# One-stream SwiGLUs with a normalized operand of 256 columns from the tenth pair, two passes in the last, and operands at multiples of 256 bytes

## The chip, the cores and the metric

One NeuronCore of one Trainium2 chip runs the whole program in a single launch. The metric is device microseconds of one execution.

## The reference, cut to what matters

A stream x of 256 tokens by 1,024 channels and a context of 256 tokens go through two layers. Layer 0: a half-step SwiGLU on both streams, a mixer (windowed attention and a gated linear attention), a half-step SwiGLU on x alone. Layer 1: SwiGLU, pooling mixer, SwiGLU, all on x alone. So there are four SwiGLUs, the first with two streams, the second, third and fourth with one:

```
modulate(z, g, shift, scale) = rmsnorm(z, g) * (1 + scale) + shift
a, u   = split(modulate(x, ...) @ wi)      # wi: 1024 x 5632
x      = x + 0.5 * gate * ((silu(a) * u) @ wo)   # wo: 2816 x 1024
```

Shift, scale and gate are rows of `silu(c) @ w_mod + b_mod`, nine per layer. Everything is float32.

## The kernel before, in words

Channels lie on the partitions, tokens along the free dimension. A float32 product is made of float32r ones: each operand is split into a rounded part (hi, or X0) and the rest (lo, or X1), and hi·X0 + hi·X1 + lo·X0 is summed in PSUM. `weight` (line 138) loads a block of weights into `t_raw` on SP's queue, casts it to `t_hi` on ScalarE (144) and subtracts to get `t_lo` on VectorE (145); there are four buffers of each.

The first product of a SwiGLU runs in 22 *pairs*: pair p has two weight blocks of 128 x 1,024, one for a and one for u, and each goes through eight k-blocks of 128 channels. Three functions issue these matmuls:

- `product` (323): three matmuls of 258 columns per k-block. The operand `t_xA` holds x·(1 + scale)·g, not yet divided by its rms, in rows of 260 columns (NS); columns 256 and 257 hold the shift. After the pair `scaled` (375) multiplies both PSUM results by `t_rstd`, and `swiglu` (366, 367) adds the shift's products.
- `wide` (343 to 345): three matmuls of 512 columns, for two streams side by side.
- `merged` (337, 338): two passes. One matmul of 512 columns, hi·[X0 | X1], and one of 256, lo·X0, added onto the second half; `residual` adds the halves up. The second product of the one-stream SwiGLUs and the mixer's output use it.

`parts` (370, 371) splits the result into `t_g`, the operand of the second product: eight output blocks n, each over 22 k-blocks.

The first SwiGLU does the pairs in halves. In its second half it uses a *normalized* operand: `normalize` (298 to 304) multiplies two channel blocks by rstd on VectorE, scales and shifts on ScalarE, casts and subtracts into a `paired_tile`, whose k-blocks are 520 columns apart. `wide` then needs no `scaled`.

Beside this, `mod_dot` (174) computes the modulation rows with one VectorE dot per 128 rows of `w_mod`. How many dots a pair or an output block takes is set by the tables RATES0 to RATES3 through `step_mod` (187), which also issues their loads. The order of each engine's instructions is that of a scheduler in the tile framework, which places them by priority and dependence; each engine then runs its list in order.

Of the kernel before, what the change touches and what calls it, by code (L numbers as in the profile page):

```python
# [106 lines left out]
class Body:  # L107
# [270 lines left out]
    def ffn(self, l, wi, wo, Xs, rstds, gate, streams, nxt, rates, first=None):  # L378
# [7 lines left out]
        if first is None:
            cmg, gp = self.open(f"g{self.uid}", "right")
            self.modpool = gp
        for h in range(nh):
            G = None if first is not None and h == 0 else self.t(gp, [128, pph, 2, W], F32R, "g")  # L390
            split = first is not None and h == 0
            if split:
                cme, ep = self.open("early", "right")
                early = [self.t(ep, [128, 2, T], F32) for _ in range(pph)]
                begin, weights, pair, during, second, norm = first
                nf = begin(early)
                self.step_mod(rates[0][0])
                w = weights(nf)
                for p in range(nf, pph):
                    ps = [self.bank(), self.bank()]  # L400
                    pair(p, w, ps)
                    if p + 1 < pph:
                        w = weights(p + 1)
                    for q in (0, 1):
                        nc.scalar.copy(early[p][:, q, :], ps[q][:, :T])
                    during(p)
                    self.step_mod(rates[0][0])
                rstds = second()
                cmg, gp = self.open(f"g{self.uid}")
                self.modpool = gp  # L410
                G = self.t(gp, [128, pph, 2, W], F32R, "g")
            for j in range(pph):
                p = h * pph + j
                w = [self.weight(wi[p, i], 1024) for i in (0, 1)]
                if first is not None and not split:
# [11 lines left out]
                for i in range(ns):  # L427
                    self.step_mod(rates[h][1] / ns if 0 < j < pph - 1 else 0)
                    if i == 0 and split:
                        continue  # L430
                    c = slice(i * T, (i + 1) * T)
                    ps = [self.bank(), self.bank()]
                    for q in (0, 1):
                        self.product(ps[q], w[q], Xs[i])
                    if callable(rstds):
                        rstds = rstds()
                    za = self.scaled(gp, ps[0], rstds[i], T + 1, "za")
                    zu = self.scaled(gp, ps[1], rstds[i], T + 1, "zu")
                    if split:
                        e = early[p]  # L440
                        be = self.t(gp, [128, 2], F32, "be", 2)
                        for q in (0, 1):
                            nc.scalar.copy(be[:, q:q + 1], ps[q][:, T + 1:T + 2])
# [816 lines left out]
```

## Time and profile before

| | |
|---|---|
| median of 3 runs | 1169.08 us (1167.88 to 1169.91) |
| profiled execution, its own time | 1165.99 us |
| its span, first to last instruction | 1163.8 us |
| mean granted TensorE clock | 0.998 |
| busy share: PE, PEld, VectorE, ScalarE | 98%, 89%, 81%, 49% |

PE is TensorE's matmuls, PEld its weight loads, DVE is VectorE, ACT ScalarE, SP the engine whose queue issues the DMAs. Matmuls are pipelined, so that their durations overlap; L328 is line 328 of the kernel before.

### The profile page before, as it was taken

How to read it: one execution, taken by the hardware profiler on the slowest of the kernel's cores; microseconds unless marked ns; L12 is line 12 of the kernel's file. 1: busy time of each engine (PE TensorE's matmuls, PEld its weight loads, DVE VectorE, ACT ScalarE, POOL GpSimd, SP SyncE). 2: the span in 40 equal slices, each digit the busy share in tenths (PEclk: the TensorE clock that was granted, in tenths of full speed). 3: DMA queues.
4: the chain of work that ended last, by engine and by line, in shares of the span. 5: the costliest groups of instructions: out<-in, count | busy, mean ns of one | idle time of the engine just before them, and what ended most of it. 6: DMA issues, size and time to landing. Idle time of an engine off the chain costs nothing.

```text
span 1163.8 us, 19972 instructions
## 1 busy us (share of the span) xinstructions
PE 1142.5 (98%) x7658; PEld 1039.4 (89%) x7658; DVE 946.0 (81%) x1690; ACT 574.1 (49%) x937; POOL 10.0 (1%) x32
## 2 busy tenths in 40 slices
PE   7999999999999999999999999999999999999997
PEld 5999988888888899787999998899999889999986
DVE  6899799788758889776998878989887989966564
ACT  4647544232234464565555544545554455555543
POOL 0000000000000200000000000000000000000000
PEclk9999999999999999999999999999999999999999
DMA  8866557667755435311678767978776876655562
GB/s 341 296 249 226 160 186 232 201 200 264 249 162 194 167 108 176 118 66 60 236 265 266 253 205 249 321 268 303 255 256 193 301 251 230 219 182 177 150 185 87
DMA packets 74546, 247.45 MB, mean 213 GB/s; under 512 B 8273, under 2 KB 8913, under 8 KB 74194
## 3 DMA queue, kind: packets, MB, share of 16 engines
...
q14 instruction: 36, 0.29, 0.1%
...
## 4 chain that ended last, share of the span: by engine, by line
PE 92%; DVE 5%; DMA 1%; ACT 1%; issue 1%; SPq 0%; DVEq 0%; ACTq 0%
PE t_mm L330 15%; PE t_mm L329 15%; PE t_mm L328 15%; PE t_mm L337 11%; PE t_mm L343 7%; PE t_mm L345 7%; PE t_mm L344 7%; PE t_mm L338 6%; PE t_mm L582 3%; PE t_mm L903 1%; PE t_mm L876 1%; DVE t_lo L145 1%; PE t_mm L893 1%; DMA t_raw<-wi0k 1%; PE t_mm L626 1%
## 5 line engine op out<-in xcount | busy, mean ns | idle before, releaser
L144 ACT CAST t_hi<-t_raw 128x1024 fp32r<-128x1024 f32 (+1 forms) x344 | 326.6, 951 | 416.7 <-PE t_mm L329 175.1
L328 PE MATMUL t_mm<-t_xA,t_hi 128*128 128x258 f32 (+1 forms) x1536 | 437.4, 285 | 3.3 <-DVE t_x L929 2.1
L330 PE MATMUL t_mm<-t_xA,t_lo 128*128 128x258 f32 (+1 forms) x1536 | 437.6, 285 | 1.6 <-DVE t_lo L145 1.6
L329 PE MATMUL t_mm<-t_xA,t_hi 128*128 128x258 f32 (+1 forms) x1536 | 434.8, 283 | 0.1
L145 DVE TENSOR_TENSOR t_lo<-t_raw,t_hi 128x1024 fp32r<-128x1024 f32 (+1 forms) x344 | 376.6, 1097 | 70.9 <-ACT t_hi L144 70.0
L328 PEld LDWEIGHTS t_mm<-t_xA,t_hi 128*128 128x128 f32 x1536 | 292.3, 191 | 6.5 <-DVE t_x L929 2.4
L329 PEld LDWEIGHTS t_mm<-t_xA,t_hi 128*128 128x128 f32 x1536 | 291.3, 190 | 2.3 <-issue 1.4
L330 PEld LDWEIGHTS t_mm<-t_xA,t_lo 128*128 128x128 f32 x1536 | 290.9, 189 | 2.0 <-DVE t_lo L145 2.0
L174 DVE CUSTOM_DVE_ANT_0 t_junk<-t_rawm,t_x 128x1024 bf16<-128x1024 f32 x142 | 181.7, 1279 | 16.4 <-DMA t_rawm<-wmod 15.6
L337 PE MATMUL t_mm<-t_g,t_hi 128*128 128x512 f32 x528 | 185.8, 394 | 0.0
L338 PE MATMUL t_mm<-t_g,t_lo 128*128 128x256 f32 x528 | 147.5, 279 | 0.0
L337 PEld LDWEIGHTS t_mm<-t_g,t_hi 128*128 128x128 f32 x528 | 99.0, 187 | 23.4
L338 PEld LDWEIGHTS t_mm<-t_g,t_lo 128*128 128x128 f32 x528 | 99.1, 188 | 0.0
L343 PE MATMUL t_mm<-t_xA,t_hi 128*128 128x512 f32 x176 | 69.7, 396 | 0.0
L345 PE MATMUL t_mm<-t_xA,t_lo 128*128 128x512 f32 x176 | 69.6, 396 | 0.0
L344 PE MATMUL t_mm<-t_xA,t_hi 128*128 128x512 f32 x176 | 69.2, 393 | 0.0
L343 PE MATMUL t_mm<-t_g,t_hi 128*128 128x512 f32 x176 | 68.6, 390 | 0.0
L344 PE MATMUL t_mm<-t_g,t_hi 128*128 128x512 f32 x176 | 68.5, 389 | 0.0
L345 PE MATMUL t_mm<-t_g,t_lo 128*128 128x512 f32 x176 | 68.5, 389 | 0.0
L375 DVE TENSOR_TENSOR t_zu<-t_mm,t_rstd 128x257 f32<-128x257 f32 x66 | 27.9, 425 | 28.8 <-PE t_mm L330 28.6
L366 ACT ACTIVATE t_za<-t_za 128x256 f32<-128x256 f32 x77 | 38.6, 508 | 14.5 <-DVE t_za L375 14.4
L174 DVE CUSTOM_DVE_ANT_0 t_junk<-t_w,t_x 128x1024 bf16<-128x1024 f32 x32 | 41.0, 1281 | 4.6 <-DMA t_w<-wmod 2.9
...
## 6 DMA issues: line engine op xcount, KB each, us to landing
...
```

Source lines behind the costliest of these rows:

```text
L144: nc.scalar.copy(hi[:, :n], raw[:, :n])
L145: self.mark = nc.vector.tensor_tensor(lo[:, :n], raw[:, :n], hi.bitcast(F32)[:, :n], op=ALU.subtract)
L174: self.nc.vector.tensor_tensor_reduce(out=junk, in0=w, in1=self.srow[s], scale=0.5 if half else 1.0, scalar=b, op0=ALU.mult, op1=ALU.add, ...
L328: nc.tensor.matmul(ps[:, :n], hi[:, c], X[:, 0, k, :n], start=(k == 0), stop=False)
L329: nc.tensor.matmul(ps[:, :n], hi[:, c], X[:, 1, k, :n], start=False, stop=False)
L330: nc.tensor.matmul(ps[:, :n], lo[:, c], X[:, 0, k, :n], start=False, stop=(k == KB - 1))
L337: nc.tensor.matmul(ps, hi, X.rearrange("p x t -> p (x t)"), start=first, stop=False)
L338: nc.tensor.matmul(ps[:, T:], lo, X[:, 0], start=False, stop=last)
L343: nc.tensor.matmul(ps, hi, X0, start=first, stop=False)
L344: nc.tensor.matmul(ps, hi, X1, start=False, stop=False)
L345: nc.tensor.matmul(ps, lo, X0, start=False, stop=last)
L366: self.silu = self.nc.scalar.activation(za, za, AF.Silu, bias=ba)
```

## The change

`ffn` is split into `ffn_two` (the first SwiGLU, its work as before) and `ffn_one` (the others). In `ffn_one` pairs 0 to 8 use `product` as before. During pairs 0 to 3 the operand is also normalized, two k-blocks a pair, into a `paired_tile`. From pair 9 (OLD) on the normalized operand is used: in the second and third SwiGLU with `wide` on 256 columns, in the fourth (fold) with `merged`, whose halves are then added by a ScalarE copy and a VectorE add. Silu and the product follow without rstd or shift. Modulation dots start at pair 5 at 1.35 a pair (0.9 in the fourth), and 1.4 go to an output block. The `paired_tile` is packed: its k-blocks lie 512 columns (2,048 bytes) apart instead of 520. A pad of 24 columns in the pool of `t_g` moves that tile: in the built program of before it starts 96 bytes past a multiple of 256, now at a multiple of 256. In the first SwiGLU `t_g` starts at a multiple of 256 in both.

```diff
-RATES1 = ((0, 0.85, 1.8),)
-RATES2 = ((0, 0.85, 1.8),)
-RATES3 = ((0, 0.9, 0),)
+RATES = ((1.35, 1.4), (1.35, 1.4), (0.9, 0))
+OLD = 9
+GPAD = 24
...
     def paired_tile(self):
         f = self.t(self.xp, [128, 2 * KB * NS], F32R, "xA", 2)
-        return f.rearrange("p (k n) -> p k n", k=KB)[:, :, :2 * T].rearrange("p k (x t) -> p k x t", t=T)
+        return f[:, :2 * KB * T].rearrange("p (k x t) -> p k x t", k=KB, t=T)
...
+    def ffn_one(self, l, wi, wo, cur, gate, nxt, rates, fold):
+        nc = self.nc
+        cmg, gp = self.open(f"g{self.uid}", "right")
+        self.modpool = gp
+        G = self.t(gp, [128, NP, 2, T], F32R, "g")
+        self.t(gp, [128, GPAD], F32, "pad")
+        for p in range(NP):
+            w = [self.weight(wi[p, i], 1024) for i in (0, 1)]
+            self.step_mod(rates[0] if OLD - 4 <= p < NP - 1 else 0)
+            ps = [self.bank(), self.bank()]
+            if p < OLD:
+                for q in (0, 1):
+                    self.product(ps[q], w[q], cur.X[0])
+                if p == 0:
+                    r = cur.stats()[0]
+                    XN = self.paired_tile()
+                za = self.scaled(gp, ps[0], r, T + 1, "za")
+                zu = self.scaled(gp, ps[1], r, T + 1, "zu")
+                self.swiglu(za[:, :T], za[:, :T], zu[:, :T], za[:, T:T + 1], zu[:, T:T + 1])
+                self.parts(G, p, slice(0, T), za[:, :T])
+                if p < KB // 2:
+                    self.normalize([XN[:, 2 * p:2 * p + 2, i] for i in (0, 1)], gp, 0, 2 * p, r, cur.A[0], cur.B[0])
+                continue
+            za = self.t(gp, [128, T + 1], F32, "za", 2)[:, :T]
+            if fold:
+                zu = self.t(gp, [128, T + 1], F32, "zu", 2)[:, :T]
+            for q in (0, 1):
+                for k in range(KB):
+                    c = slice(k * 128, (k + 1) * 128)
+                    hi, lo = w[q][0][:, c], w[q][1][:, c]
+                    if fold:
+                        self.merged(ps[q], hi, lo, XN[:, k], k == 0, k == KB - 1)
+                    else:
+                        self.wide(ps[q][:, :T], hi, lo, XN[:, k, 0], XN[:, k, 1], k == 0, k == KB - 1)
+                if fold:
+                    z = (za, zu)[q]
+                    nc.scalar.copy(z, ps[q][:, :T])
+                    nc.vector.tensor_tensor(z, z, ps[q][:, T:], op=ALU.add)
+            self.silu = nc.scalar.activation(za, za if fold else ps[0][:, :T], AF.Silu)
+            nc.vector.tensor_tensor(za, za, zu if fold else ps[1][:, :T], op=ALU.mult)
+            self.parts(G, p, slice(0, T), za)
+        nxt.begin()
...
-        self.ffn(0, a["wi1"], a["wo1"], cur.X, cur.stats, 8, (0,), nxt, RATES1)
+        self.ffn_one(0, a["wi1"], a["wo1"], cur, 8, nxt, RATES[0], False)
...
-        self.ffn(1, a["wi2"], a["wo2"], cur.X, cur.stats, 2, (0,), nxt, RATES2)
+        self.ffn_one(1, a["wi2"], a["wo2"], cur, 2, nxt, RATES[1], False)
...
-        self.ffn(1, a["wi3"], a["wo3"], nxt.X, nxt.stats, 8, (0,), fin, RATES3)
+        self.ffn_one(1, a["wi3"], a["wo3"], nxt, 8, fin, RATES[2], True)
```

Where instructions move. VectorE's list in the second SwiGLU, before, from the conversion of pair 4's first weight (`t1121_lo`) to that of its second (`t1124_lo`); `t1083_za` and `t1084_zu` are pair 0's, `t1093_za` and `t1094_zu` pair 1's:

```order
L145 TENSOR_TENSOR t1121_lo_5948<-t1119_raw_5946,t1120_hi_5947 128x1024
L214 SCALAR_TENSOR_TENSOR t1082_rstd_t_5708<-t1082_rstd_t_5708,t1080_rv_5705 128x256
L201 SCALAR_TENSOR_TENSOR t1332_x_7269<-t816_x_4396,t4_x_78 128x1
L215 SCALAR_TENSOR_TENSOR t1081_rstd_5707<-t1082_rstd_t_5708,t1081_rstd_5707 128x256
L375 TENSOR_TENSOR t1083_za_5720<-t1077_mm_5653,t1081_rstd_5707 128x257
L375 TENSOR_TENSOR t1084_zu_5722<-t1078_mm_5654,t1081_rstd_5707 128x257
L375 TENSOR_TENSOR t1093_za_5790<-t1091_mm_5740,t1081_rstd_5707 128x257
L375 TENSOR_TENSOR t1094_zu_5792<-t1092_mm_5741,t1081_rstd_5707 128x257
L145 TENSOR_TENSOR t1124_lo_5954<-t1122_raw_5952,t1123_hi_5953 128x1024
```

The same list of the changed kernel, up to the conversion of pair 4's second weight, now `t1126_lo` (its first, `t1123_lo`, stands 11 rows ahead of the first row here). `t1107_za` is pair 2's, `t1118_za` and `t1119_zu` are pair 3's, L297 and L303 are the multiply and the subtraction of `normalize`:

```order
L370 TENSOR_TENSOR t1068_g_5636<-t1096_za_5798,t1068_g_5636 128x256
L297 TENSOR_TENSOR t1109_xt_5882<-t5_x_80,t1082_rstd_5708 128x512
L303 TENSOR_TENSOR t1084_xA_5721<-t1098_xt_5806,t1084_xA_5721 128x2x256
L366 SCALAR_TENSOR_TENSOR t1107_za_5874<-t1108_zu_5876,t1107_za_5874 128x256
L374 TENSOR_TENSOR t1118_za_5950<-t1116_mm_5900,t1082_rstd_5708 128x257
L374 TENSOR_TENSOR t1119_zu_5952<-t1117_mm_5901,t1082_rstd_5708 128x257
L370 TENSOR_TENSOR t1068_g_5636<-t1107_za_5874,t1068_g_5636 128x256
L297 TENSOR_TENSOR t1120_xt_5958<-t5_x_80,t1082_rstd_5708 128x512
L366 SCALAR_TENSOR_TENSOR t1118_za_5950<-t1119_zu_5952,t1118_za_5950 128x256
L303 TENSOR_TENSOR t1084_xA_5721<-t1109_xt_5882,t1084_xA_5721 128x2x256
L145 TENSOR_TENSOR t1126_lo_5972<-t1124_raw_5970,t1125_hi_5971 128x1024
```

The conversion has moved behind pair 3's `t_zu` and behind the normalizing of pairs 0 to 2.

PE's list in the fourth SwiGLU at the step from pair 8 to pair 9, before:

```order
L328 MATMUL t2009_mm_10997<-t1877_xA_10256,t2005_hi_10989 128x258
L329 MATMUL t2009_mm_10997<-t1877_xA_10256,t2005_hi_10989 128x258
L330 MATMUL t2009_mm_10997<-t1877_xA_10256,t2006_lo_10990 128x258
L328 MATMUL t2019_mm_11068<-t1877_xA_10256,t2013_hi_11055 128x258
L329 MATMUL t2019_mm_11068<-t1877_xA_10256,t2013_hi_11055 128x258
L330 MATMUL t2019_mm_11068<-t1877_xA_10256,t2014_lo_11056 128x258
```

And of the changed kernel:

```order
L327 MATMUL t2012_mm_11069<-t1869_xA_10242,t2008_hi_11061 128x258
L328 MATMUL t2012_mm_11069<-t1869_xA_10242,t2008_hi_11061 128x258
L329 MATMUL t2012_mm_11069<-t1869_xA_10242,t2009_lo_11062 128x258
L336 MATMUL t2021_mm_11138<-t1922_xA_10521,t2016_hi_11127 128x512
L337 MATMUL t2021_mm_11138<-t1922_xA_10521,t2017_lo_11128 128x256
```

From pair 9 on, a k-block takes two matmuls and two weight loads instead of three, on another `t_xA` tile.

## Rows read from the trace of the kernel before

**Rows 1.** The page, busy time: us, share of the span, number of instructions.

```profile
PE 1142.5 (98%) x7658; PEld 1039.4 (89%) x7658; DVE 946.0 (81%) x1690; ACT 574.1 (49%) x937; POOL 10.0 (1%) x32
```

**Rows 2.** The page, the chain that ended last, shares of the span by engine and by line.

```profile
PE 92%; DVE 5%; DMA 1%; ACT 1%; issue 1%; SPq 0%; DVEq 0%; ACTq 0%
PE t_mm L330 15%; PE t_mm L329 15%; PE t_mm L328 15%; PE t_mm L337 11%; PE t_mm L343 7%; PE t_mm L345 7%; PE t_mm L344 7%; PE t_mm L338 6%; PE t_mm L582 3%; PE t_mm L903 1%; PE t_mm L876 1%; DVE t_lo L145 1%; PE t_mm L893 1%; DMA t_raw<-wi0k 1%; PE t_mm L626 1%
```

**Rows 3.** The waits of PE from 556 to 1160 us: us in total, times, the longest.

```profile
PE t_mm L260 <- DVE t_ss L276: 1.4, 1, 1.4
PE t_mm L1162 <- ACT t_sq L1147: 1.3, 1, 1.3
PE t_mm L328 <- ACT t_xA L319: 1.2, 3, 0.5
PE t_mm L330 <- DVE t_lo L145: 0.4, 1, 0.4
```

**Rows 4.** Line 343 on PE in the first SwiGLU (the first matmul of three in `wide`), from 150 to 260 us and from 200 to 340 us: count, duration in ns (least, median, most), first and last start in us. `t_g` in the second product's first half, `t_xA` in the first product's second half.

```profile
L343 PE MATMUL t_mm<-t_g,t_hi x88: 388/389/398, 150.6 to 209.8; 128*128 128x512 f32 x88
...
L343 PE MATMUL t_mm<-t_xA,t_hi x176: 387/396/400, 210.5 to 332.5; 128*128 128x512 f32 x176
```

**Rows 5.** Line 328 on PE (the first of three in `product`) in stretches of the second, third and fourth SwiGLU, and early in the first with 256 columns; columns as in rows 4.

```profile
L328 PE MATMUL t_mm<-t_xA,t_hi x204: 279/282/288, 605.9 to 679.9; 128*128 128x258 f32 x102
...
L328 PE MATMUL t_mm<-t_xA,t_hi x210: 277/282/285, 800.0 to 874.8; 128*128 128x258 f32 x105
...
L328 PE MATMUL t_mm<-t_xA,t_hi x220: 279/282/288, 1005.0 to 1084.7; 128*128 128x258 f32 x110
...
L328 PE MATMUL t_mm<-t_xA,t_hi x37: 275/279/285, 47.9 to 60.7; 128*128 128x256 f32 x37
```

**Rows 6.** Line 337 on PE (the first of two in `merged`) in the second product of the second and the third SwiGLU; columns as in rows 4.

```profile
L337 PE MATMUL t_mm<-t_g,t_hi x161: 391/393/395, 699.7 to 755.7; 128*128 128x512 f32 x161
...
L337 PE MATMUL t_mm<-t_g,t_hi x152: 392/393/395, 891.9 to 944.7; 128*128 128x512 f32 x152
```

**Rows 7.** Groups by line and shape over the whole span: count, busy us, mean ns of one, idle us before them and what ended it. The conversion on VectorE, the dot, `scaled`, the two of `normalize`, the product and the subtraction of a pair.

```profile
L145 DVE TENSOR_TENSOR t_lo<-t_raw,t_hi 128x1024 fp32r<-128x1024 f32 x216 | 263.1, 1221 | 30.4 <-ACT t_hi L144 29.7
...
L174 DVE CUSTOM_DVE_ANT_0 t_junk<-t_rawm,t_x 128x1024 bf16<-128x1024 f32 x142 | 181.7, 1279 | 16.4 <-DMA t_rawm<-wmod 15.6
...
L367 DVE SCALAR_TENSOR_TENSOR t_za<-t_zu,t_za 128x256 f32<-128x256 f32 x66 | 31.5, 484 | 5.6 <-DVE t_zu L375 0.5 <-ACT t_za L366 0.4
...
L375 DVE TENSOR_TENSOR t_zu<-t_mm,t_rstd 128x257 f32<-128x257 f32 x66 | 27.9, 425 | 28.8 <-PE t_mm L330 28.6
...
L371 DVE TENSOR_TENSOR t_g<-t_za,t_g 128x256 fp32r<-128x256 f32 x66 | 27.3, 418 | 0.1
...
L174 DVE DVE_READ_ACCUMULATOR2_ANT t_x<- 128x1 f32 x184 | 15.1, 82 | 0.0
...
L304 DVE TENSOR_TENSOR t_xA<-t_xt,t_xA 128x512 fp32r<-128x512 f32 x8 | 5.5, 686 | 0.4 <-ACT t_xA L303 0.4
L298 DVE TENSOR_TENSOR t_xt<-t_x,t_rs 128x512 f32<-128x512 f32 x8 | 5.4, 685 | 0.0
```

**Rows 8.** VectorE in order of time at the start of the second SwiGLU: start us, us, instruction. The last row is the conversion of pair 4's second weight.

```profile
585.26 0.43 DVE L375 TENSOR_TENSOR t_za<-t_mm,t_rstd 128x257 f32<-128x257 f32 x1
585.61 0.42 DVE L375 TENSOR_TENSOR t_zu<-t_mm,t_rstd 128x257 f32<-128x257 f32 x1
585.94 0.42 DVE L375 TENSOR_TENSOR t_za<-t_mm,t_rstd 128x257 f32<-128x257 f32 x1
...
586.60 1.22 DVE L145 TENSOR_TENSOR t_lo<-t_raw,t_hi 128x1024 fp32r<-128x1024 f32 x1
```

**Rows 9.** PE in order of time: the first matmul with the converted rest (`t_lo`) of pair 4's first and of its second weight, in the second SwiGLU; of the second weight in the third SwiGLU; of pair 3's second and of pair 4's first in the fourth.

```profile
590.88 0.29 PE L330 MATMUL t_mm<-t_xA,t_lo 128*128 128x258 f32 x1
...
593.79 0.29 PE L330 MATMUL t_mm<-t_xA,t_lo 128*128 128x258 f32 x1
...
783.71 0.28 PE L330 MATMUL t_mm<-t_xA,t_lo 128*128 128x258 f32 x1
...
989.53 0.29 PE L330 MATMUL t_mm<-t_xA,t_lo 128*128 128x258 f32 x1
...
992.45 0.29 PE L330 MATMUL t_mm<-t_xA,t_lo 128*128 128x258 f32 x1
```

**Rows 10.** VectorE in order of time at the start of the third SwiGLU: two modulation dots and the conversion of pair 4's second weight.

```profile
767.83 1.28 DVE L174 CUSTOM_DVE_ANT_0 t_junk<-t_rawm,t_x 128x1024 bf16<-128x1024 f32 x1
...
774.15 1.28 DVE L174 CUSTOM_DVE_ANT_0 t_junk<-t_rawm,t_x 128x1024 bf16<-128x1024 f32 x1
...
781.15 1.21 DVE L145 TENSOR_TENSOR t_lo<-t_raw,t_hi 128x1024 fp32r<-128x1024 f32 x1
```

**Rows 11.** Two stretches, the start of the second SwiGLU and its second product: from and to, us, busy us and instructions of each engine, granted clock, mean busy share of the DMA engines, GB/s.

```profile
572.00:600.00 28.00, 28.00 (x232) 27.94 (x231) 27.53 (x51) 14.89 (x21) 0.00 (x0) 1.00 0.73 250
720.00:750.00 30.00, 30.00 (x173) 26.13 (x172) 27.95 (x48) 15.45 (x24) 0.00 (x0) 1.00 0.94 324
```

More of the change, by code (lines that the diff above doesn't have):

```diff
@@ L376, in scaled, with ffn_two @@
         return z
-    def ffn(self, l, wi, wo, Xs, rstds, gate, streams, nxt, rates, first=None):
+    def ffn_two(self, wi, wo, Xs, gate, nxt, rates, first):
         nc = self.nc
-        ns = len(Xs)
-        W = T * ns
-        nh = 2 if ns == 2 else 1
+        W, nh = 2 * T, 2
         pph = NP // nh
-        if first is None:
-            cmg, gp = self.open(f"g{self.uid}", "right")
-            self.modpool = gp
-        for h in range(nh):
[L390 to L411, printed above, removed]
+        begin, weights, pair, during, second, norm = first
+        cme, ep = self.open("early", "right")
+        early = [self.t(ep, [128, 2, T], F32) for _ in range(pph)]
+        nf = begin(early)
+        self.step_mod(rates[0][0])
+        w = weights(nf)
+        for p in range(nf, pph):
+            ps = [self.bank(), self.bank()]
+            pair(p, w, ps)
+            if p + 1 < pph:
+                w = weights(p + 1)
+            for q in (0, 1):
+                nc.scalar.copy(early[p][:, q, :], ps[q][:, :T])
+            during(p)
+            self.step_mod(rates[0][0])
+        rstds = second()
+        cmg, gp = self.open(f"g{self.uid}")
+        self.modpool = gp
+        for h in range(nh):
+            G = self.t(gp, [128, pph, 2, W], F32R, "g")
             for j in range(pph):
@@ L414, in ffn @@
                 w = [self.weight(wi[p, i], 1024) for i in (0, 1)]
-                if first is not None and not split:
-                    self.step_mod(rates[h][1] if 0 < j < pph - 1 else 0)
-                    ps = [self.bank(), self.bank()]
+                self.step_mod(rates[h][1] if 0 < j < pph - 1 else 0)
+                ps = [self.bank(), self.bank()]
+                if h:
                     for q in (0, 1):
@@ L426, in ffn @@
                     continue
[L427 to L443, printed above, removed]
-                        nc.vector.tensor_tensor(e, e, rstds[0][:, :T].unsqueeze(1).to_broadcast([128, 2, T]),
-                                                op=ALU.mult)
-                        self.swiglu(e[:, 0, :], e[:, 0, :], e[:, 1, :], be[:, 0:1], be[:, 1:2])
-                        self.swiglu(e[:, 1, :], za[:, :T], zu[:, :T], za[:, T:T + 1], zu[:, T:T + 1])
-                        self.mark = self.parts(G, j, slice(0, W), e.rearrange("p q t -> p (q t)"))
-                        continue
-                    self.swiglu(za[:, :T], za[:, :T], zu[:, :T], za[:, T:T + 1], zu[:, T:T + 1])
-                    self.parts(G, j, c, za[:, :T])
@@ L452, in ffn @@
-            if split:
-                self.close(cme)
-            parts = WO_PARTS[2 * h:2 * h + 2] if ns == 2 else WO_PARTS
-            last = h == nh - 1
-            if last:
-                nxt.begin()
-            elif first is not None:
+                for q in (0, 1):
+                    self.product(ps[q], w[q], Xs[1])
+                za = self.scaled(gp, ps[0], rstds[1], T + 1, "za")
+                zu = self.scaled(gp, ps[1], rstds[1], T + 1, "zu")
+                e = early[p]
@@ L459, in ffn @@
+            parts = WO_PARTS[2 * h:2 * h + 2]
+            if h:
+                nxt.begin()
+            else:
+                self.close(cme)
                 cmy, yp = self.open("half", "right")
```

74 lines of the change are left out of this document (45 added, 29 removed).

## The prediction

> **What bounds the kernel now.** I read the page first. TensorE is busy 98% of the span, VectorE 81%, ScalarE 49% [rows 1]. The chain that ended last is 92% PE, its costliest lines are the matmuls of `product`, `merged` and `wide`, and VectorE is 5% of it, in the mixer and the pool mixer [rows 2]. The waits of PE over the four SwiGLUs' one-stream part (556 to 1160 us) are next: a handful of waits, the longest on a converted weight 0.4 us, once [rows 3]. So in every SwiGLU the time is a number of matmuls times the interval from one matmul's start to the next. A matmul's duration in the profile (some 0.28 us) is no such interval, since matmuls overlap. The interval is read from the first and the last start of a line in a stretch, and the count.
>
> The intervals do not follow the columns alone. `wide` with 512 columns takes (209.8 - 150.6) / 87 = 0.6805 us for its three matmuls when the operand is the two-stream `t_g`, and (332.5 - 210.5) / 175 = 0.6971 us when it is the normalized operand in `t_xA` [rows 4]: 226.8 against 232.4 ns for the same instruction. What differs in the program is the address: `t_g` lies in rows of 2,048 bytes and starts at a multiple of 256, the rows in `t_xA` are 2,080 bytes apart. The one-stream `t_g` also has rows of 2,048 bytes, but starts 96 bytes past a multiple of 256, and its 512 + 256 columns take 56.0 / 160 = 0.350 us [rows 6]. `product` with 258 columns takes 74.0 / 203 = 0.3645 us for three matmuls in the second SwiGLU, 74.8 / 209 = 0.3579 in the third, 79.7 / 219 = 0.3639 in the fourth; with 256 columns of the same layout, early in the first, 12.8 / 36 = 0.3556 [rows 5].
>
> **The change part by part.** Below, "triple" is hi·X0, hi·X1, lo·X0 of one weight block.
>
> 1. *Rows of 2,048 bytes for the paired operand (first SwiGLU, second half).* 176 triples go from 0.6971 to the 0.6805 that aligned rows show: 176 x 0.0166 = 2.9 us. Bounds: 0 if the address is not the cause, 2.9.
>
> 2. *The one-stream `t_g` at a multiple of 256, and `merged` in the mixer's output.* 528 + 64 blocks at 0.350 us. I scale by the ratio that 512 columns show, 0.6805 / 0.6971 = 0.976: 0.3416 us, 592 x 0.0084 = 5.0 us. Bounds: 0; and 226.8 + 113.4 = 0.3402 us, if 256 aligned columns cost half of 512, which gives 5.8.
>
> 3. *Pairs 9 to 21 of the second and third SwiGLU with 256 aligned columns.* No row shows 256 columns from an aligned `t_xA`. From above, 0.3556 (unaligned rows); from below, 3 x 113.4 = 0.3402. I take 0.3556 x 0.976 = 0.3471, in the middle, since the ratio is measured and the half is not. 13 x 16 = 208 triples each: 208 x (0.3645 - 0.3471) + 208 x (0.3579 - 0.3471) = 3.6 + 2.2 = 5.9 us. Bounds: 2.3 and 8.7.
>
> 4. *Pairs 9 to 21 of the fourth with two passes.* 208 triples of 0.3639 become 208 blocks of 0.3416: 4.6 us. Bounds: 2.9 (blocks at 0.350) and 4.9.
>
> Sum of the gains on PE: 2.9 + 5.0 + 5.9 + 4.6 = 18.4 us; with every lower bound 5.2, with every upper 22.4.
>
> The Trainium skill (SBUF — State Buffer, Specifications (TRN2)) speaks against the parts on alignment: it gives lines of 16 bytes, with a penalty where an access crosses to a new one. Row steps of 2,080 and 1,040 bytes and a start 96 bytes past 256 are all multiples of 16, so by it parts 1 and 2 are nothing and the sum is the lower one, 5.2 us; rows 4 disagree with it, but don't name the cause.
>
> 5. *What VectorE must do more, and when.* Pairs 0 to 3 of each one-stream SwiGLU get the normalizing: on VectorE two operations of 512 elements, 0.69 us each [rows 7], on ScalarE two activations and a cast. 4 x 1.37 = 5.5 us more there. In exchange no modulation dot runs before pair 5 (one costs 1.28 + 0.08 us); before, three run there. ScalarE at about half load covers its share. VectorE is busy 27.5 of 28 us there already [rows 11], so the order counts. In the second SwiGLU, VectorE's list puts the conversion of pair 4's second weight behind pair 3's `t_zu`, which needs the end of pair 3 on PE; before, it stood ahead of that and ran at 586.60 [rows 8]. PE starts pair 4 with the matmuls around 590.88 and wants that weight at 593.79 [rows 9]. From 590.9: `t_zu` 0.33, sub 0.33, the 512-element multiply 0.65, product 0.40, the 512-element sub 0.65, the conversion 1.21 (the durations of rows 7, less the 0.03 to 0.09 us by which neighbours overlap, as in rows 8): ready at 594.5, a new wait of 0.7 us. In the third, 4.3 us of operations come between the end of the rstd chain and that conversion (four multiplies and two subs of 0.65, one product of 0.40), and two dots of 1.28 go. Before it ran at 781.15 and ended at 782.36 [rows 10], PE wanted it at 783.71 [rows 9]: ready at 784.1 if the dots' time comes back in full, 786.7 if not at all. I take 1.5 us of wait. In the fourth, the conversion of pair 4's first weight stands behind pair 3's `t_za`, which needs the first half of that pair on PE, to 989.5: with `t_za` 0.33, multiply 0.65, sub 0.33 and itself 1.21 it is ready at 992.0, wanted at 992.45 [rows 9]; I take no wait. Together 2.2 us lost; bounds 0.4 and 5.
>
> 6. *Costed at nothing.* From pair 9 VectorE does two conversions (2.44), one multiply from PSUM (0.43), one sub (0.42) and 1.35 dots (1.84): 5.1 us in a pair of 16 x 0.347 = 5.55 us; before 5.35 in 5.83. So the cover stays as thin as it was; what would uncover it is a late conversion, and that is D below. In the fourth SwiGLU the two added sums bring VectorE to 4.2 us in 5.47. In the output products 1.4 dots a block replace 1.8: VectorE's 27.95 of 30 us [rows 11] is 7.2 in a block of 7.7, and becomes 6.6 in 22 x 0.3416 = 7.5. The modulation loads move along with their dots in SP's queue; weight and modulation loads together go to (2 + 1.35) x 0.524 MB in 5.55 us, 317 GB/s; a stretch with 324 GB/s had PE busy without a gap [rows 11]. What a load waits for in that queue is its raw buffer, and that comes free with the conversions of part 5.
>
> Net: 18.4 - 2.2 = 16.2 us. The profiled execution took 1165.99 us (its span 1163.8 and 2.2 around it), so 1149.8 there; the median of the runs shown is 3.1 us above it, so **1152.9 us** on that scale.
>
> **The rivals.**
>
> *A, the forecast:* as above, own range 1147 to 1160 (gains of 22.4 with 0.4 lost; gains of 11.8, half of the alignment, with 3 lost). For it: the same instruction at 226.8 and 232.4 ns, each over 88 triples and more. Chance 0.80.
>
> *B, alignment does nothing:* `t_g` of the first SwiGLU is quicker for another reason, and the change doesn't do what it says. For it: the first row of `t_xA` is aligned already, and the third SwiGLU's `product` is 2.2 ns per matmul quicker than the second's with the same layout, so the place in memory matters in ways that rows 5 don't explain. Then 5.2 - 2.2 = 3.0: 1166.1 us. The skill's 16-byte lines lead here. Chance 0.10.
>
> *C, only columns count:* from 118.5 ns at 256 and 232.4 at 512 columns a column is 0.445 ns; two columns off 1,248 matmuls are 1.1 us, six off 208 blocks 0.6; less 2.2: 1169.6 us. Against it: the 0.0090 us between the triples of 258 and 256 columns is over three times that, and `merged` at 0.350 is measured. Chance 0.05. The Trainium skill (TensorE: Matmul & The Clock Gate, Back-to-back issue gap) has such a rule, N / 2.4 GHz plus 2.5 ns, which makes 110.0, 109.2 and 215.8 ns of 258, 256 and 512 columns and 2.0 us of the whole change; the trace's 121.5, 118.5 and 232.4 ns, at a granted clock of 1.00, are above it.
>
> *D, VectorE becomes the bound at the start of each SwiGLU:* the place is pairs 0 to 8. If all the normalizing is waited for, 3 x 5.5 = 16.4 us, and also the dots of pairs 5 to 8 (1.35 for 0.85, 2 x 4 x 0.5 x 1.28 = 5.1), 21.5 us are lost: 1169.1 - 18.4 + 21.5 = 1172.2 us, slower. It decides once the lost time passes 18.4, some 6 us a SwiGLU. For it: the lead of the conversions falls to a few us there, and the only wait of PE on a weight is there. Against it: the dots that leave, and the leads that must be eaten first, 6.0 us before that conversion in the second SwiGLU and 1.3 in the third [rows 8 to 10]. Chance 0.05.
>
> **How the numbers follow.** The point is A's. The range goes from 1146, A's lower end less half the 2.0 us over which the runs shown spread, to 1166, which takes in B's time less a little; C and D lie outside. 0.2% is 2.3 us, about what a measurement of this kernel can tell from no change. Faster by more: A and half of B and a bit, 0.86. Within: C and the rest of B, 0.08. Slower: D, and C with more stalls, 0.06.
>
> **What would show it.** Triples of line `wide` at 0.68 us on `t_xA` in the first SwiGLU; blocks of 0.342 in the three output products; triples of 0.347 from pair 9 in the second and third SwiGLU, blocks of 0.342 in the fourth; PE waiting for `t_lo` some 2 us in all around pair 4 of the second and third. Unaligned intervals (0.697, 0.350, 0.356) would prove B; waits on `t_lo` of over 5 us in a SwiGLU would prove D, and PE idle on a weight's load would be a case that I have not priced.

## The result and the profile after

The changed kernel takes 1161.49 us (median of 4 runs, 1161.40 to 1162.19) against 1168.48 for the kernel before (1167.64 to 1169.91): a ratio of 0.994, 95% interval 0.9923 to 0.9957, 7.0 us faster. The forecast was 1152.9, 16.2 us faster. The sign and the range held; the size did not.

The page of the changed kernel: busy time by engine, and the chain that ended last.

```profile
PE 1137.5 (98%) x7450; PEld 1027.0 (89%) x7450; DVE 938.5 (81%) x1662; ACT 587.4 (51%) x999; POOL 9.9 (1%) x32
...
PE 86%; DVE 7%; DMA 3%; ACT 2%; issue 2%; SPq 0%; DVEq 0%; ACTq 0%
```

PE still bounds it [rows 1, 2]. So the time again lies in intervals and counts. Matmuls on PE in the changed kernel, columns as in rows 4: `wide` with 512 columns in the first SwiGLU, with 256 in the second and third, `merged` in their output products, then `merged` in the fourth, on `t_xA` and in two output blocks.

```profile
L342 PE MATMUL t_mm<-t_xA,t_hi x174: 389/389/389, 213.0 to 330.6; 128*128 128x512 f32 x174
...
L342 PE MATMUL t_mm<-t_xA,t_hi x201: 283/283/283, 619.9 to 691.9; 128*128 128x256 f32 x101
...
L342 PE MATMUL t_mm<-t_xA,t_hi x204: 283/283/283, 808.8 to 881.9; 128*128 128x256 f32 x102
...
L336 PE MATMUL t_mm<-t_g,t_hi x171: 395/398/403, 694.7 to 754.8; 128*128 128x512 f32 x171
...
L336 PE MATMUL t_mm<-t_g,t_hi x171: 395/398/403, 883.7 to 943.7; 128*128 128x512 f32 x171
...
L336 PE MATMUL t_mm<-t_xA,t_hi x203: 392/395/395, 1015.9 to 1085.9; 128*128 128x512 f32 x102
...
L336 PE MATMUL t_mm<-t_g,t_hi x21: 395/398/476, 1118.1 to 1125.2; 128*128 128x512 f32 x21
...
L336 PE MATMUL t_mm<-t_g,t_hi x22: 391/391/476, 1126.1 to 1133.4; 128*128 128x512 f32 x22
```

Three matmuls of 512 columns take 117.6 / 173 = 0.680 us, as forecast. Three of 256 take 72.0 / 200 = 0.3600, not 0.347: 0.0045 less than the 258 columns that they replace in the second SwiGLU, and 0.0021 more than those in the third [rows 5]. A block of 512 + 256 in the output products takes 60.1 / 170 = 0.3535, *more* than the 0.350 at the unaligned address [rows 6]; in the fourth SwiGLU's pairs it takes 70.0 / 202 = 0.3465. The last two rows are neighbouring output blocks with the same operand: the durations, 398 and 391 ns at the median, show that one chain runs at two paces.

The stages, cut at the same matmul of both profiles (us, from the starts in the two traces):

| stage | before | after | difference | forecast |
|---|---|---|---|---|
| start and first SwiGLU up to 1st output half | 150.59 | 152.41 | +1.82 | 0 |
| first SwiGLU, `wide` on `t_xA` | 122.74 | 119.68 | -3.06 | -2.9 |
| output products: mixer, 2nd, 3rd, 4th | 39.26, 61.60, 61.84, 62.92 | 39.14, 62.19, 62.42, 62.54 | -0.12, +0.59, +0.58, -0.38 | -5.0 |
| pairs 9 to 21: 2nd, 3rd | 75.75, 74.53 | 74.87, 74.88 | -0.88, +0.34 | -5.9 |
| pairs 9 to 21: 4th | 75.75 | 72.11 | -3.63 | -4.6 |
| pairs 0 to 8: 2nd, 3rd, 4th | 53.94, 52.15, 55.04 | 54.49, 52.23, 55.88 | +0.55, +0.09, +0.84 | +2.2 |
| pool mixer and the step to the fourth | 14.83 | 13.96 | -0.86 | 0 |
| second output half, mixer, end | 203.0 | 202.6 | -0.5 | 0 |

The sum is -4.6: the profiled executions took 1165.99 and 1161.40. The first row is not the change's: the same stage took 150.59, 152.27 and 151.69 us in three executions of the kernel before. The other 2.4 us up to the medians lie in the profiled execution of before, which was a quick one (below).

The waits of PE from 540 to 1160 us, columns as in rows 3; then the two longest on a converted weight, PE in order of time, with the idle time in brackets.

```profile
PE t_mm L329 <- DVE t_lo L145: 1.4, 3, 0.6
...
PE t_mm L327 <- ACT t_xA L318: 1.0, 2, 0.5
PE t_mm L260 <- DVE t_ss L276: 0.6, 1, 0.6
```

```profile
592.34 0.39 PE L329 MATMUL t_mm<-t_xA,t_lo 128*128 128x258 f32 x1 [0.44 <-DVE t_lo L145]
...
986.16 0.38 PE L329 MATMUL t_mm<-t_xA,t_lo 128*128 128x258 f32 x1 [0.62 <-DVE t_lo L145]
```

The first is pair 4's second weight in the second SwiGLU, where the forecast put a wait; the second is pair 4's first in the fourth, where it put none.

### The profile page after: what moved, and what is told of

Its sections match the earlier page's. It is cut to its first block, busy times and chain, and to the rows that moved or that the text cites. A ratio compares the mean times of both kernels' runs of the same rounds, so it can differ in the third digit from the quotient of the medians.

```text
span 1159.2 us, 19546 instructions
## 1 busy us (share of the span) xinstructions
PE 1137.5 (98%) x7450; PEld 1027.0 (89%) x7450; DVE 938.5 (81%) x1662; ACT 587.4 (51%) x999; POOL 9.9 (1%) x32
## 4 chain that ended last, share of the span: by engine, by line
PE 86%; DVE 7%; DMA 3%; ACT 2%; issue 2%; SPq 0%; DVEq 0%; ACTq 0%
PE t_mm L336 15%; PE t_mm L342 11%; PE t_mm L344 11%; PE t_mm L343 11%; PE t_mm L337 8%; PE t_mm L329 7%; PE t_mm L328 7%; PE t_mm L327 7%; PE t_mm L610 2%; DVE t_lo L145 1%; PE t_mm L931 1%; PE t_mm L904 1%; DVE t_junk L174 1%; DMA t_x<-ctxT 1%; ACT t_hi L144 1%
## 5 line engine op out<-in xcount | busy, mean ns | idle before, releaser
L327 PE MATMUL t_mm<-t_xA,t_hi 128*128 128x258 f32 (+1 forms) x912 | 261.0, 287 | 2.7 <-DVE t_x L957 1.6
L329 PE MATMUL t_mm<-t_xA,t_lo 128*128 128x258 f32 (+1 forms) x912 | 259.6, 285 | 3.1 <-DVE t_lo L145 3.1
L328 PE MATMUL t_mm<-t_xA,t_hi 128*128 128x258 f32 (+1 forms) x912 | 258.1, 283 | 0.1
L336 PE MATMUL t_mm<-t_g,t_hi 128*128 128x512 f32 x528 | 186.6, 398 | 0.0
L344 PE MATMUL t_mm<-t_xA,t_lo 128*128 128x256 f32 (+1 forms) x592 | 186.2, 315 | 0.0
L342 PE MATMUL t_mm<-t_xA,t_hi 128*128 128x256 f32 (+1 forms) x592 | 186.2, 315 | 0.0
L343 PE MATMUL t_mm<-t_xA,t_hi 128*128 128x256 f32 (+1 forms) x592 | 186.2, 315 | 0.0
L327 PEld LDWEIGHTS t_mm<-t_xA,t_hi 128*128 128x128 f32 x912 | 173.0, 190 | 5.9 <-DVE t_x L957 1.9
L329 PEld LDWEIGHTS t_mm<-t_xA,t_lo 128*128 128x128 f32 x912 | 172.6, 189 | 4.2 <-DVE t_lo L145 4.2
L328 PEld LDWEIGHTS t_mm<-t_xA,t_hi 128*128 128x128 f32 x912 | 172.7, 189 | 2.4 <-issue 1.4
L343 PEld LDWEIGHTS t_mm<-t_xA,t_hi 128*128 128x128 f32 x592 | 112.9, 191 | 6.9
L344 PEld LDWEIGHTS t_mm<-t_xA,t_lo 128*128 128x128 f32 x592 | 112.9, 191 | 6.9
L342 PEld LDWEIGHTS t_mm<-t_xA,t_hi 128*128 128x128 f32 x592 | 112.9, 191 | 6.7
L336 PE MATMUL t_mm<-t_xA,t_hi 128*128 128x512 f32 x272 | 95.4, 396 | 0.0
L337 PE MATMUL t_mm<-t_xA,t_lo 128*128 128x256 f32 x272 | 75.4, 278 | 0.0
L342 PE MATMUL t_mm<-t_g,t_hi 128*128 128x512 f32 x176 | 68.5, 389 | 0.0
```

What stands on the lines that cost most here:

```text
L327: nc.tensor.matmul(ps[:, :n], hi[:, c], X[:, 0, k, :n], start=(k == 0), stop=False)
L328: nc.tensor.matmul(ps[:, :n], hi[:, c], X[:, 1, k, :n], start=False, stop=False)
L329: nc.tensor.matmul(ps[:, :n], lo[:, c], X[:, 0, k, :n], start=False, stop=(k == KB - 1))
L336: nc.tensor.matmul(ps, hi, X.rearrange("p x t -> p (x t)"), start=first, stop=False)
L337: nc.tensor.matmul(ps[:, T:], lo, X[:, 0], start=False, stop=last)
L342: nc.tensor.matmul(ps, hi, X0, start=first, stop=False)
```

## The experiments

Each ratio below is to the kernel before, run beside it on the same chip; medians that were not taken side by side are not compared to less than 2 us. The theories: **P**, the forecast's (an aligned operand saves 2.4% at any width); **L** (from a multiple of 256 bytes a matmul starts columns / 2.4 GHz + 13.3 ns after the one ahead, so 512 columns gain and 256 don't); **S** (a chain has two lasting paces).

**The disputed interval by itself.** `m1_intervals`: two fixed weights, one operand tile, chains like this one and like `merged`, with nothing beside them, in outline:

```
for i in range(22):        # n columns, row step 2048 bytes, start address off
    matmul(ps[:, :n], hi[:, c], X[off + k * step], ...)
    matmul(ps[:, :n], hi[:, c], X[off + k * step + x1], ...)
    matmul(ps[:, :n], lo[:, c], X[off + k * step], ...)
```

> Nothing of the model is computed here: only chains of matmuls with two fixed weights, 44 to 72 blocks for each combination of columns, start address and row step, with no load, VectorE or ScalarE work beside them. Theory L (the changed kernel's trace: from an address at a multiple of 256 a matmul takes its columns at 2.4 GHz plus 13.3 ns): 512 columns 226.7 ns, 256 columns 120.0, 258 columns 120.8, 320 columns 146.7, 192 columns 93.3, all constant from one to the next; a block of 512 + 256 takes 346.7 or 353.3 ns. Away from 256 bytes 512 columns take 230 to 234, 256 columns 117 to 120, a block of 512 + 256 350. Theory P (the forecast's: time in proportion to columns, alignment saves 2.4% at any width): 256 columns from an aligned address 113 to 116, a block of 512 + 256 340 to 342; then the 120.0 of the changed kernel comes from what runs beside it.

First matmul of three, columns as in rows 4: 256 columns at 0, at 32 and at 96 bytes past a multiple of 256, 258 at 0 and at row steps of 1,040, 512 at 0 and at 32, 192 and 320 at 0. Then the first of `merged`'s two, at 0, in two stretches.

```profile
L33 PE MATMUL t_s256o<-t_X,t_hi x31: 283/283/283, 12.9 to 23.7; 128*128 128x256 f32 x31
...
L33 PE MATMUL t_s256o<-t_X,t_hi x42: 280/280/280, 24.8 to 39.3; 128*128 128x256 f32 x42
...
L33 PE MATMUL t_s256o<-t_X,t_hi x42: 281/282/285, 55.9 to 70.6; 128*128 128x256 f32 x42
...
L33 PE MATMUL t_s258o<-t_X,t_hi x40: 283/283/283, 87.7 to 101.8; 128*128 128x258 f32 x40
...
L33 PE MATMUL t_s258p<-t_X,t_hi x42: 280/282/287, 350.0 to 364.9; 128*128 128x258 f32 x42
...
L33 PE MATMUL t_s512o<-t_X,t_hi x40: 389/389/389, 168.1 to 194.6; 128*128 128x512 f32 x40
...
L33 PE MATMUL t_s512o<-t_X,t_hi x42: 393/395/397, 196.7 to 225.4; 128*128 128x512 f32 x42
...
L33 PE MATMUL t_n<-t_X,t_hi x41: 272/273/278, 397.4 to 410.9; 128*128 128x192 f32 x41
...
L33 PE MATMUL t_n<-t_X,t_hi x41: 309/309/309, 474.1 to 491.7; 128*128 128x320 f32 x41
```

```profile
L44 PE MATMUL t_g<-t_X,t_hi x63: 391/391/391, 543.9 to 565.4; 128*128 128x512 f32 x63
...
L44 PE MATMUL t_gc<-t_X,t_hi x64: 395/398/403, 798.8 to 821.1; 128*128 128x512 f32 x64
```

At 0, three matmuls of 256 take 10.8 / 30 = 0.360 us, of 512 26.5 / 39 = 0.679, of 320 17.6 / 40 = 0.440: 120.0, 226.7 and 146.7 ns each, L's figures. At 32, 256 columns take 14.5 / 41 = 0.354 and 512 take 28.7 / 41 = 0.700: the address that costs 512 columns 2.9% *gives* 256 columns 1.8%. P is refuted without VectorE, loads or ScalarE beside it. L missed at 192 columns, 13.5 / 40 = 0.338, 112 ns instead of 93.3; 224 and 240 columns took 112 as well, and 448 took 206.7 instead of 200.0: the form holds at 256, 320, 384 and 512 columns, not at every width. 258 columns take 14.1 / 39 = 0.361 at 0 and 14.9 / 41 = 0.363 at row steps of 1,040. The same chain of 512 + 256 took 21.5 / 62 = 0.347 in one stretch and 22.3 / 63 = 0.354 in another.

**The pad taken out.** `GPAD` and its tile left out; `t_g` is 96 bytes off again.

> The changed kernel without the pad, so that the one-stream t_g starts 96 bytes past a multiple of 256 again. Theory L: blocks of the output products go from 353.3 back to 350.1 ns in the second and third SwiGLU (352 x 3.2 ns = 1.1 us gained) and from a mean of 349 to 350.5 in the fourth (0.3 us lost): 0.8 us faster than the changed kernel, 1160.7. Theory P: the pad was worth 528 x 8.4 ns = 4.4 us: 1165.9.

Line 336 in the second and third SwiGLU's output products:

```profile
L336 PE MATMUL t_mm<-t_g,t_hi x172: 392/393/397, 692.8 to 752.7; 128*128 128x512 f32 x172
...
L336 PE MATMUL t_mm<-t_g,t_hi x170: 392/394/398, 882.7 to 941.8; 128*128 128x512 f32 x170
```

59.9 / 171 = 0.3503 and 59.1 / 169 = 0.3497. 1160.76 us, ratio to before 0.9931 (0.9908 to 0.9953): no slower without the pad. P's 1165.9 is outside.

**Alignment alone, without the normalized operand.** On the kernel before:

```diff
-        return f.rearrange("p (k n) -> p k n", k=KB)[:, :, :2 * T].rearrange("p k (x t) -> p k x t", t=T)
+        return f[:, :2 * KB * T].rearrange("p (k x t) -> p k x t", k=KB, t=T)
...
+                self.t(gp, [128, 24], F32, "pad")
```

> The kernel before with the packed paired operand and a pad that brings t_g to a multiple of 256, and nothing else. Theory L: 2.9 us gained in the first SwiGLU, 64 x 3 ns = 0.2 in the mixer's output, 1.1 lost in the output products of the second and third: 2.0 faster than before, some 1166.4. Theory P: 2.9 + 5.0 = 7.9 faster, 1160.6.

Line 337 in the same two output products:

```profile
L337 PE MATMUL t_mm<-t_g,t_hi x172: 392/394/395, 695.7 to 755.0; 128*128 128x512 f32 x172
...
L337 PE MATMUL t_mm<-t_g,t_hi x171: 395/398/403, 883.7 to 943.7; 128*128 128x512 f32 x171
```

1166.31 us against 1167.9, ratio 0.9976 (0.996 to 0.9992): 1.6 us faster (0.9 to 4.7 by the interval): L's 2.0 lies in it and P's 7.9 does not. The second SwiGLU now runs at 59.3 / 171 = 0.3468 and the third at 0.3529, at one address, as S has it.

**Two passes in all three** (`True` for `fold` in the two other calls).

> The changed kernel with two passes in the second and third SwiGLU too (fold in all three), the modulation dots as they are. Theory L: on PE 416 blocks go from 360.0 to 346.7 ns, 5.5 us gained: 1156 if VectorE keeps up. VectorE does two sums more a pair, 5.1 + 0.84 = 5.95 us against PE's 5.55: if it becomes the bound, 26 pairs of 5.95 instead of 5.76: 4.9 us lost, 1166.4, with PE waiting for a converted weight or a bank. Theory P: 347.1 to 341.6, 2.3 us gained at most.

1156.11 us, ratio 0.9894 (0.9863 to 0.9925), on L's sum. Pairs 9 to 21 of the second took 72.11 us instead of 74.87, of the third 73.48 instead of 74.88 (the slow pace). VectorE kept up: no wait on a weight in these pairs.

**What picks the pace.** `m2_states` and two more executions of the kernel before.

> Chains of matmuls alone again, nothing of the model: 44 blocks of 512 + 256 from each of eight start addresses (0, 32, ... 224 bytes past a multiple of 256, row step 2,048), each behind a chain of 258-column triples of 8, 9, 11, 14 or 16 k-blocks, so five times with another lead. Theory S (two lasting states): at 0 a stretch takes either 346.7 or 353.3 ns a block from its first blocks to its last, and which one depends on what ran ahead; at other addresses the states are others, or one. Theory T (what VectorE, ScalarE and the loads do beside it makes the difference): without such work all five stretches of an address agree.

Per block of 512 + 256, in ns, from the starts in the trace, five stretches each:

| bytes past 256 | 0 | 32 | 64 | 96 | 128 | 160 | 192 | 224 |
|---|---|---|---|---|---|---|---|---|
| quickest | 346.6 | 346.7 | 353.2 | 350.0 | 350.9 | 346.7 | 353.3 | 346.7 |
| slowest | 353.1 | 346.7 | 353.3 | 350.1 | 351.2 | 346.8 | 353.3 | 353.4 |

Two stretches at 0 and two at 32:

```profile
L44 PE MATMUL t_ma<-t_X,t_hi x41: 391/391/391, 158.9 to 172.7; 128*128 128x512 f32 x41
...
L44 PE MATMUL t_ma<-t_X,t_hi x41: 395/398/403, 308.6 to 322.8; 128*128 128x512 f32 x41
...
L44 PE MATMUL t_mb<-t_X,t_hi x43: 390/390/394, 29.8 to 44.4; 128*128 128x512 f32 x43
...
L44 PE MATMUL t_mb<-t_X,t_hi x44: 390/390/403, 327.8 to 342.8; 128*128 128x512 f32 x44
```

At 0 one stretch of five ran at the slow pace, from its first blocks to its last, behind a lead of another length (durations 395/398/403 instead of 391); at 224 three of five did, at 32 and 160 none of ten. With nothing beside the chains the stretches of one address disagree, so theory T falls. Each lead ran once, so this does not tell the lead from chance. The multiple of 256 was not the best address for two passes, nor for 256 columns.

> The kernel before, unchanged, for its profile in another execution. Theory S: where its time differs from 1165.99 us, whole stretches differ by a step (product's triple 0.3584 or 0.3642, a block of 512 + 256 0.3500 or 0.3508), above all the third SwiGLU's 352 triples, worth 2.0 us. Rival: the difference lies in the loads at the start and in the two mixers.

> The kernel before once more, unchanged. Theory S: it differs from the other executions by whole stretches at another step, 2.0 us for each SwiGLU whose product triples take 0.3642 instead of 0.3584. Rival: by loads and mixers.

They took 1171.12 and 1170.60 us. Line 328 in the third SwiGLU, the stretch of rows 5, in the one and in the other; then a wait of PE in the first of them, and a stretch behind that wait in the first, in the second and in the profile of before (columns as in rows 11, the granted clock third from the end):

```profile
L328 PE MATMUL t_mm<-t_xA,t_hi x207: 280/282/287, 799.9 to 874.9; 128*128 128x258 f32 x104
```

```profile
L328 PE MATMUL t_mm<-t_xA,t_hi x206: 280/282/287, 800.0 to 874.7; 128*128 128x258 f32 x103
```

```profile
PE t_mm L260 <- DVE t_ss L276: 2.3, 1, 2.3
```

```profile
956.00:958.00 2.00, 2.00 (x12) 2.00 (x11) 1.16 (x4) 0.00 (x0) 0.00 (x0) 0.50 0.20 37
```

```profile
954.00:957.00 3.00, 3.00 (x16) 3.00 (x16) 2.45 (x10) 0.56 (x1) 0.00 (x0) 0.50 0.26 101
```

```profile
951.00:954.00 3.00, 3.00 (x25) 2.92 (x24) 2.40 (x10) 1.11 (x2) 0.00 (x0) 1.00 0.25 91
```

75.0 / 206 = 0.364 where the profile of before had 0.3579: the third SwiGLU's quicker `product`, which I could not explain, was the quick pace of one execution. Pairs 0 to 21 of the third are 1.7 and 2.2 us longer than in the profile of before, and the pool mixer's stage 2.4 and 1.7. Of the latter, 0.8 and 0.2 are a longer wait for the sum of squares (2.3 and 1.6 us instead of 1.4 [rows 3]). The rest is the clock: 1.6 and 0.9 us after PE went on, the granted clock fell to 0.50, the level of 1.2 GHz, for about 3 us, and from the wait's end to the first matmul of the fourth SwiGLU PE took 12.2 and 12.1 us, where the profile of before, with the clock at 1.00, has 10.6. The changed kernel, whose wait there is 0.6 us, shows no such fall. The third SwiGLU (S) and the pool mixer (the rival) are most of the 4.6 to 5.1 us; the start has another 1.7 and 1.1. So the profile from which I worked was a quick execution; these two are slower than the median beside them, 1168.39, so a usual one lies between, and against it the change saves more than 4.6.

**256 columns, 32 bytes off.** `paired_tile(8)` in `ffn_one`: the operand starts 8 columns later.

> The changed kernel with the one-stream normalized operand starting 32 bytes past a multiple of 256 instead of at it (row steps 2,048 bytes as before). Theory L with the first measurement of chains alone: 256 columns go from 360.0 to 353.4 ns a triple in pairs 9 to 21 of the second and third SwiGLU, 416 x 6.6 ns = 2.7 us gained; the two passes of the fourth stay at 346.7 or go to 353: 1158.7 us (1160.1 with the latter). Theory P: alignment lost, 2.4% slower: 416 x 8.4 + 208 x 8.4 ns = 5 us, 1166.7.

Line 342 in the second and third:

```profile
L342 PE MATMUL t_mm<-t_xA,t_hi x202: 278/278/278, 620.7 to 691.8; 128*128 128x256 f32 x101
...
L342 PE MATMUL t_mm<-t_xA,t_hi x201: 278/278/278, 809.0 to 879.7; 128*128 128x256 f32 x101
```

71.1 / 201 = 0.3537 and 0.3535, from 0.3600. 1157.58 us (1154.48 to 1159.78), ratio 0.9896 (0.9873 to 0.9918): faster than the changed kernel's 0.994, as L has it and against P.

**The dots put back.** The forecast's fifth step said that VectorE gives with the dots what it takes with the normalizing.

```diff
-RATES = ((1.35, 1.4), (1.35, 1.4), (0.9, 0))
+RATES = ((0.85, 1.8), (0.85, 1.8), (0.9, 0))
-            self.step_mod(rates[0] if OLD - 4 <= p < NP - 1 else 0)
+            self.step_mod(rates[0] if 0 < p < NP - 1 else 0)
```

> The changed kernel with the modulation dots where the kernel before had them in the second and third SwiGLU (0.85 a pair from pair 1 on, 1.8 an output block). The forecast's fifth step: three dots of 1.28 us come back to the pairs in which the operand is normalized, some 4 us of VectorE work a SwiGLU, and PE waits for t_lo there up to 3 us longer in each; and the sum of squares at the third's end comes 1 us later for the pool mixer: 1164 to 1169. Rival: VectorE has time for both there: within 1 us of the changed kernel.

The waits of PE from 540 to 1160 us that grew; VectorE's conversion in the third SwiGLU and PE's matmul that waited for it; and what came behind (from and to, us, busy us and instructions of each engine, granted clock, DMA share, GB/s):

```profile
PE t_mm L329 <- DVE t_lo L145: 4.6, 5, 2.8
PE t_mm L327 <- ACT t_hi L144: 2.1, 2, 1.2
PE t_mm L260 <- DVE t_ss L276: 1.6, 1, 1.6
```

```profile
785.98 1.22 DVE L145 TENSOR_TENSOR t_lo<-t_raw,t_hi 128x1024 fp32r<-128x1024 f32 x1
...
787.25 0.39 PE L329 MATMUL t_mm<-t_xA,t_lo 128*128 128x258 f32 x1 [2.78 <-DVE t_lo L145]
```

```profile
787.00:788.00 1.00, 0.75 (x6) 0.75 (x7) 1.00 (x3) 1.00 (x2) 0.00 (x0) 1.00 0.00 0
788.00:789.00 1.00, 1.00 (x8) 1.00 (x7) 1.00 (x3) 1.00 (x2) 0.00 (x0) 0.63 0.71 147
789.00:790.00 1.00, 1.00 (x6) 1.00 (x6) 1.00 (x3) 0.33 (x2) 0.00 (x0) 0.50 1.14 356
790.00:791.00 1.00, 1.00 (x7) 1.00 (x6) 0.81 (x1) 0.23 (x1) 0.00 (x0) 0.50 0.65 119
791.00:792.00 1.00, 1.00 (x7) 1.00 (x7) 0.39 (x2) 0.60 (x1) 0.00 (x0) 0.66 0.78 270
```

1170.65 us, *slower than before* and above the 1164 to 1169 expected: ratio 1.003 (1.0014 to 1.0045). Against the changed kernel pairs 0 to 8 are 2.4, 4.8 and 1.2 us longer, the pool mixer 1.0. In the third, PE stood 2.8 us for one conversion, and about 1 us after it went on the granted clock fell to 0.50, the level of 1.2 GHz, for about 3 us: matmuls started 215 ns apart instead of 120, some 1.5 us more.

**Three edits together.** Two passes in all three, the normalized operand from pair 6, both one-stream operands 32 bytes past 256 (`OLD = 6`, `GPAD = 16`, `paired_tile(8)`, dots from pair 5 as in the change); and the same with `NS = 264`.

> The changed kernel with two passes in all three one-stream SwiGLUs, the normalized operand from pair 6 instead of 9, and both one-stream operands 32 bytes past a multiple of 256, where chains alone took 346.7 ns a block in 10 stretches of 10. Against the changed kernel: 2 x 208 x 13.3 ns = 5.5 us in pairs 9 to 21 of the second and third SwiGLU, 9 x 16 x 17.5 = 2.5 in pairs 6 to 8 of the three, 352 x 6.6 = 2.3 and 0.2 in the output products: 10.5 faster, 1151.0. Rival: VectorE (two sums more a pair) or the operand's completion becomes the bound from pair 6 on, PE waits for t_lo, a bank or t_xA: 1153 to 1156.

> The same with the rows of t_xA 264 columns (1,056 bytes) apart instead of 260 (1,040), so that every row of product starts at a multiple of 32 bytes. Chains of 258 columns alone took 360.0, 360.0, 356.0, 360.2 and 359.9 ns a triple at 0, 32, 64, 96 and 128 bytes, and 364 at row steps of 1,040. If that holds for rows at mixed addresses: some 4.5 ns for each of 464 triples in the SwiGLUs and about 190 in the mixer, 2.9 us, against the kernel without it. Rival: mixed addresses are the reason of the 364, not their multiple of 16: no difference.

Line 336 of the first kernel in the second SwiGLU, on `t_xA` and on `t_g`, and line 327 in the first SwiGLU; then line 327 there in the second kernel:

```profile
L336 PE MATMUL t_mm<-t_xA,t_hi x250: 390/390/391, 600.6 to 686.9; 128*128 128x512 f32 x125
...
L336 PE MATMUL t_mm<-t_g,t_hi x169: 390/390/391, 689.7 to 747.9; 128*128 128x512 f32 x169
...
L327 PE MATMUL t_mm<-t_xA,t_hi x135: 280/282/288, 99.9 to 148.7; 128*128 128x258 f32 x135
```

```profile
L327 PE MATMUL t_mm<-t_xA,t_hi x138: 279/282/288, 99.7 to 148.9; 128*128 128x258 f32 x138
```

1150.07 us (1149.82 to 1150.23), ratio 0.9837 (0.9823 to 0.9852): every chain of 512 + 256 in the one-stream SwiGLUs at 0.3467, and the four runs 0.4 us apart, where 17 runs of before lay between 1164.1 and 1171.2. With rows of 1,056 bytes the triple goes from 48.8 / 134 = 0.364 to 49.2 / 137 = 0.359 as expected; 1149.18 us (1148.57 to 1150.57), ratio 0.9832 (0.9817 to 0.9847), 0.9 less where 2.9 was expected, and not told apart by the intervals. Its four runs, with the operands at the same offsets, lie 2.0 us apart: that the offset narrows the spread of the times is not shown.

**One number on the kernel before**, `NS = 264`, nothing else.

> The kernel before with one number changed: rows of t_xA 264 columns (1,056 bytes) apart instead of 260 (1,040); nothing of the change. With the 359.3 ns a triple of 258 columns that such rows showed, against 364.2 (358.4 in the third SwiGLU of one execution): 1,440 triples x 4.9 ns = 7.1 us, 5 if the third was quick already; and the first SwiGLU's 512 columns, whose rows then start at 0, 64, 128 or 192 bytes past 256 (680, 687, 700 ns a triple in chains alone at the first three) go from 697 to some 690, 1.2 us: 1160 to 1163, as much as the whole change gave. Rival: the 359.3 belongs to what else was different there (fewer product pairs, other neighbours): 1168.5 as before.

Line 328 in the second and the third SwiGLU, and line 343 on `t_xA` in the first:

```profile
L328 PE MATMUL t_mm<-t_xA,t_hi x208: 279/282/288, 605.6 to 680.0; 128*128 128x258 f32 x104
...
L328 PE MATMUL t_mm<-t_xA,t_hi x210: 279/281/288, 799.9 to 875.0; 128*128 128x258 f32 x105
...
L343 PE MATMUL t_mm<-t_xA,t_hi x173: 388/395/399, 213.3 to 332.8; 128*128 128x512 f32 x173
```

74.4 / 207 = 0.3594 and 75.1 / 209 = 0.3593, but `wide` only to 119.5 / 172 = 0.695. 1164.97 us against 1170.65 beside it, ratio 0.9956 (0.994 to 0.9973): 5.7 us from one number, at the low end of the 5.5 to 8.5 expected (1160 to 1163 from 1168.5). The intervals of this ratio and of the whole change's overlap.

## Why the prediction was right in sign and wrong in size

**Part 1** was right: 3.06 us for 2.9, and `wide` at 0.680.

**Parts 2 and 3 failed at one step**: "I scale by the ratio that 512 columns show". The 13.3 ns that an aligned matmul takes over its columns at 2.4 GHz are the same at 256 and at 512 columns; I let them shrink with the columns. The rows allowed the other reading: 226.8 ns at 512 [rows 4] less 256 columns of 0.417 ns at a granted clock of 1.00 is 120, above the 118.5 of unaligned 256 columns [rows 5], so by a constant no gain was to be had there. Part 3 gave 0.5 us for 5.9. Part 2 lost 0.7 us net for a forecast gain of 5.0: by the same step the quick pace everywhere would have given only 592 x 3.3 ns = 2.0, and a second pace, which the forecast did not have, took the rest, since both output products with 176 blocks in the second and third fell into the slow one. Of the 11.6 us between forecast and profile, these two parts hold 11.1. Both bounds were wrong below: I let the price of unseen rows end at nothing or at the unaligned value, and no row excluded a loss.

**Part 4** was right as a mechanism, 3.6 us for 4.6: the block takes 0.3465, not 0.3416, by the same step.

**Part 5** was right in what kept it small: with the dots back it is 8.4 us more. Its sum, 1.5 us for 2.2, was right in part by luck. By place it was right once in three: 0.55 in the second (0.7), 0.1 in the third (1.5: the conversion ended at 780.39, 1.8 us ahead of PE), 0.8 in the fourth (none). In the fourth I also read the rows one pair late: the last two of rows 9, at 989.53 and 992.45, belong to pair 4's second weight and pair 5's first, and pair 4's first was wanted at 986.62. Both ends of that sum shift alike, so this is not why the wait was missed. **Part 6** was right: no wait on a weight from pair 9 on.

**Not in the forecast**: the pool mixer's start, 0.9 us earlier, because 1.4 dots a block leave VectorE less behind at the third's last block (the wait for the sum of squares is 0.6 us instead of 1.4 [rows 3]; 1.6 with 1.8 dots a block). And the base: an execution with the third SwiGLU at its quick pace and no fall of the clock in the pool mixer.

**The rivals.** B's mechanism fell with part 1, although its 3.0 us were nearer to the profiled 4.6 than mine. D's outcome, slower than before, came with the dots back, but not at its price: PE lost 8.4 us more in pairs 0 to 8 and 1.0 in the pool mixer, some 1.5 of it to the clock, where D wanted 18.4, and the gains against it were smaller than forecast. C fell with part 1 too. The Trainium skill (TensorE: Matmul & The Clock Gate, Back-to-back issue gap) gives for the isolated gap of one matmul the form that the chains alone show at 256, 320, 384 and 512 columns, columns at 2.4 GHz plus a constant; its constant is 2.5 ns, the traces' is 13.3 at a multiple of 256. The Trainium skill's 16-byte lines (SBUF — State Buffer, Specifications (TRN2)) don't order these runs either: row steps of 1,040 and 1,056 bytes are both multiples of 16, and differ by 5 ns a triple.

Still open: why an address sets the interval, and what picks the pace. That a chain keeps the pace in which it starts is shown. That what ran ahead picks it is argued: each lead ran once, and the kernel before ran the same list of matmuls at 0.3579 in one execution and at 0.364 in two others.
